# Transposes in place of products for row factors, a token-wise end, and an instruction order from another timing model, in a two-layer hybrid trunk

## The chip, the cores and the metric

The kernel runs on one core of a Trainium2 chip. The metric is the device time of one execution in microseconds, the median of three runs. TensorE is called PE, VectorE DVE, ScalarE ACT, GpSimd POOL, and SyncE, which issues most transfers, SP.

## What is computed

256 tokens of width 1024 pass two layers. Each layer adds half a SwiGLU step, a token mixer of four head groups (forgetting attention, retention, an SSD, HGRN2), another half SwiGLU step, and a gated embedding. The trunk ends with one norm. All of it is float32.

```
h = x
for i in range(DEPTH):
    h = h + 0.5 * swiglu(rmsnorm(h, ffn1_norm[i]), ffn1_w_up[i], ffn1_w_down[i])
    h = h + token_mixer(rmsnorm(h, mix_norm[i]), ...)
    h = h + 0.5 * swiglu(rmsnorm(h, ffn2_norm[i]), ffn2_w_up[i], ffn2_w_down[i])
    gate = sigmoid(rmsnorm(h, ple_norm[i]) @ ple_w_gate[i])
    h = h + gate * (p[i] @ ple_w_proj[i])
return rmsnorm(h, final_norm)
```

## The kernel before

The state `H` stays on the chip with the 1024 channels on the partitions (eight blocks of 128) and the 256 tokens along the free axis. A product in the accuracy that is wanted is made of three: weights and activations are each split into a high part (`wh`, `yh`, a cast on ACT, L160 and L190) and a low part (`wl`, `yl`, a subtraction on DVE, L161 and L191), and PE adds wh·yh, wh·yl and wl·yh into one bank (`prod`, L255; `token_tiles`, L287 to L289, where the tokens are on the partitions of the result).

Weights stream through: SP brings a tile of 128x1024 (`raw`, four buffers), ACT makes `wh` and DVE `wl` (eight buffers each), two tiles ahead of the use (`weight`, `AHEAD`). The banks of PSUM are `bank_p` (two), `bank_m` (two) and `bank_a` (four).

A norm (`Norm`) multiplies `H` by the norm's weights before the split, and takes the factor of each token afterwards: squares on ACT (L204), sums over the channel blocks on POOL (L206, L209), sums over the partitions on PE (L104), nine small steps on DVE for the root (L241 to L250), and then `spread` (L228), two products of the factor's column against the identity matrix, which lay the 256 factors along the free axis of all partitions. Such products in full precision, against the identity or another constant, stand in four more places: L370 (head norms), L731 and L787 (SSD), L812 (forgetting attention). L760, L857, L858 and L863 are real transposes.

In the mixer one projection makes all groups' inputs. `hf` and `hq` of HGRN come first (banks 2336 and 2337 in layer 0, 8815 and 8816 in layer 1), with the statistics of the norm among them, then `hv` and a few columns for gates (banks 2508 and 2509; 8999 and 9000), whose chain of small steps on DVE is `small` (L667 to L687, tiles `sm`), then `fv` (banks 2674 and 2675; 9165 and 9166), then the rest. The parts of the mixer are generators that a planner takes turns with; the order on each engine is then fixed by the tile context's scheduler, which weighs instructions by a timing model of its own. HGRN begins on DVE when the spread factor is there: `hf` and `hq` are scaled (L383), logarithms taken on ACT, a scan (L546), `h` for the carry `dc` (L548, L564), a diagonal product on POOL (L566), and then for each of eight levels exponents (L585 to L596 on DVE, L599 and L600 on ACT), `qt` (L613, DVE) and a product (L621 for the first two, L626 for the others), and masked copies (L637). L653 to L657 make the values. In layer 1 lower bounds add steps (L533, L534, L538, L553).

At the end of layer 1 the gate of the embedding is computed channel block by channel block (`gate`, `gated`, L977 to L980), and the final norm takes squares, statistics, the root, the spread (L228) and one product of `scaled` with the spread factor for each block (L986, L990), and SP writes the result (L991), which the host transposes.

```
    class Norm:
        def spread(self, keep=True):
            for t in range(2):
                mm(self.b[:, 256 + t * P:256 + (t + 1) * P],
                   self.col[:, t:t + 1].broadcast_to([P, P]), ident,
                   start=True, stop=True, skip_group_check=True)
```

Of the kernel before, what the change touches and what calls it, by code (L numbers as in the profile page):

```python
# [47 lines left out]
for _name, _w in (("ffn1", 8), ("mix", 8), ("ffn2", 8), ("ple", 8), ("fin", 8), ("ret", 2),  # L48
                  ("hgrn", 2), ("ssd", 2), ("cw", 16), ("cb", 4), ("lb0", 2), ("lb1", 2),
                  ("sd", 2), ("bias", 8), ("alog", 4)):  # L50
    PAR[_name] = (_n, _w)
    _n += _w
# [4 lines left out]
for _name, _w in (("ident", 128), ("cum", 256), ("cum64", 128), ("m0", 128), ("m1", 128),  # L57
                  ("m2", 128), ("tot", 128), ("cos", 256), ("sin", 256),
                  ("dec", 1024), ("lvl", 6 * 64), ("reset", 512), ("hsel", 2), ("neg", 128)):
    CON[_name] = (_n, _w)  # L60
    _n += _w
# [3 lines left out]
def trunk(ctx, tc, x, pt, par_d, con_d, w_d, ws_d, out):  # L65
# [31 lines left out]
    def flat(t):  # L97
        return t.rearrange("p a b -> p (a b)")

# [79 lines left out]
    class Norm:  # L179
        def __init__(self, split=True):  # L180
            self.split = split
            self.h, self.l, self.sq = [], [], []

        def part(self, c, l, name, first=False):
            if self.split:
                xh, xl = v2(tw("yh", F32R)), v2(tw("yl", F32R))
                for i in range(2):
                    d = 2 * c + i
                    w = prm(l, name, d)
                    A.mul(xh[:, i], H[:, d], w)  # L190
                    V.scalar_tensor_tensor(xl[:, i], H[:, d], w, xh[:, i].bitcast(F32),  # L191
                                           ALU.mult, ALU.subtract)
                    self.h.append(xh[:, i])
                    self.l.append(xl[:, i])
            if not first:
                self.square(c)

        def square(self, c):
            sq = tw("m2")
            if c == 3 and not self.split:  # L200
                for d in range(2):
                    self.last = A.activation(v2(sq)[:, d], H[:, 2 * c + d], AF.Square).ins
            else:
                A.activation(sq, flat(H[:, 2 * c:2 * c + 2]), AF.Square)  # L204
# [15 lines left out]
        def scale(self, keep=True):  # L220
            self.stats()
            self.col = rsqrt(self.b[:, 0:2], 2, 1.0 / D)
            if not keep:
                self.spread(False)

        def spread(self, keep=True):
            for t in range(2):
                mm(self.b[:, 256 + t * P:256 + (t + 1) * P],  # L228
                   self.col[:, t:t + 1].broadcast_to([P, P]), ident,
                   start=True, stop=True, skip_group_check=True)  # L230
            rb = self.b[:, 256:512]
            if keep:
                rb = cp.tile([P, S], F32, name=f"rb{cnt[0]}", tag="rb")
                A.copy(rb, self.b[:, 256:512])
            self.rb = rb.unsqueeze(1).broadcast_to([P, 2, S])
# [112 lines left out]
    def head_norm(o, gate, wname, l, kind, which):  # L348
# [351 lines left out]
    def ssd(l, got, need):  # L700
# [25 lines left out]
        for hp in range(2):  # L726
            br = bank("m")
            for hh in range(2):
                h = 2 * hp + hh
                for t in range(2):  # L730
                    mm(br[:, hh * S + t * P:hh * S + (t + 1) * P],  # L731
                       g[:, t, h:h + 1].broadcast_to([P, P]), K("cum64"), start=True, stop=True,
                       skip_group_check=True)
            br4 = br.rearrange("p (h c e) -> p h c e", h=2, c=4)
            hs = slice(2 * hp, 2 * hp + 2)
            V.tensor_tensor(a0.rearrange("p (h c e) -> p h c e", h=4, c=4)[:, hs], br4,
                            bias[:, hs, 0:4].unsqueeze(3).broadcast_to([P, 2, 4, 64]), ALU.add)
            V.tensor_tensor(a1.rearrange("p (h c e) -> p h c e", h=4, c=2)[:, hs],
                            br4[:, :, 2:4],
                            bias[:, hs, 4:6].unsqueeze(3).broadcast_to([P, 2, 2, 64]), ALU.add)  # L740
# [54 lines left out]
    def fox(l, got, need):  # L795
# [114 lines left out]
    def advance(update, l, name, split=True, first=False):  # L910
        xn = Norm(split)
# [5 lines left out]
    def hpair(c):  # L917
        return flat(H[:, 2 * c:2 * c + 2])

# [18 lines left out]
    for l in range(DEPTH):  # L938
# [8 lines left out]
        ph, pl = split(p_sb)  # L947
        wp = by_row()
# [12 lines left out]
        def gate(c):  # L961
            w = by_column()
            z = v2(tw("m2"))
            if l == DEPTH - 1 and c == 3:
                for m in range(2):
                    b = v2(bank("a"))
                    wh, wl = w[m]
                    for k in range(KD):
                        prod(b[:, 0], wh[:, k], wl[:, k], xn.h[k], xn.l[k], k == 0, k == KD - 1)
                    gated(c, z[:, m:m + 1], b[:, 0:1], m, m + 1)  # L970
            else:
                b = bank("a")
                col_tiles(((b, w),), xn, k_outer=(c == 0))
                gated(c, z, v2(b), 0, 2)

        def gated(c, z, b, m, e):
            V.tensor_mul(z, b, xn.rb[:, m:e])  # L977
            A.activation(z, z, AF.Sigmoid)
            V.tensor_mul(z, z, v2(bp[c])[:, m:e])
            V.tensor_add(H[:, 2 * c + m:2 * c + e], H[:, 2 * c + m:2 * c + e], z)  # L980

        xn = advance(gate, 1, "ffn1", split=(l == 0))
    scaled = [v2(tw("m2")) for _ in range(4)]
    with tc.issue_after(xn.last):
        for d in range(KD):
            A.mul(scaled[d // 2][:, d % 2], H[:, d], prm(1, "fin", d))  # L986
    xn.scale(keep=False)
    for c, o in enumerate(scaled):
        for m, e in ((0, 1), (1, 2)) if c == 0 else ((0, 2),):
            V.tensor_mul(o[:, m:e], o[:, m:e], xn.rb[:, m:e])  # L990
            nc.sync.dma_start(out[:, 2 * c + m:2 * c + e], o[:, m:e])  # L991


def _constants():
# [5 lines left out]
    f["cum64"] = (s <= t) & (s // 64 == t // 64)  # L1000
# [107 lines left out]
```

## Time and profile before

| | |
|---|---|
| median of three runs | 1133.43 us (1131.43 to 1135.0) |
| the profiled execution, its own time | 1132.47 us |
| its span | 1130.7 us |
| granted clock of PE, mean | 0.997 |
| PE busy | 1102.3 us, 97%, 9468 instructions |
| DVE busy | 750.5 us, 66% |
| ACT busy | 568.7 us, 50% |
| POOL busy | 42.1 us, 4% |
| transfers | 193.77 MB, 171 GB/s on average |

A page of the profile gives, engine by engine, the busy share, and in 40 slices the clock that PE was granted. The timeline has one instruction, or several of one kind, to a row: start and duration in us, engine, line, operation, output and inputs, shapes. PE's instructions overlap, so their price is the distance between starts and not the duration. In brackets stands how long the engine was idle before, and what ended that.

### The profile page before, as it was taken

The numbers are of one execution on the slowest core, as the hardware profiler recorded it, in microseconds if no ns is written. First come the engines' busy times: TensorE is split into PE (matmuls) and PEld (weight loads), VectorE is DVE, ScalarE is ACT, GpSimd is POOL, SyncE is SP. The second block draws the span as 40 slices with busy tenths as digits, with TensorE's granted clock in tenths as the row PEclk, the third lists the DMA queues.
The fourth block names the chain that finished last, engine by engine and source line by source line (L and its number), as shares of the span: only waits on it lengthen the run. The fifth ranks groups of instructions, "written<-read, shape, count | busy, mean of one in ns | idle before, by whom it ended". The sixth has DMA issues, their size and how long they took to land.

```text
span 1130.7 us, 22461 instructions
## 1 busy us (share of the span) xinstructions
PE 1102.3 (97%) x9468; PEld 1079.2 (95%) x9468; DVE 750.5 (66%) x1077; ACT 568.7 (50%) x762; POOL 42.1 (4%) x39
## 2 busy tenths in 40 slices
PE   7999999999999999999999999998999999999996
PEld 7999999879899999999999999997899999999996
DVE  6755556798769555556975555577997775555584
ACT  6544444645477444444665444446446854444453
POOL 2000000200001000000100000010000100000011
PEclk9999999999999999999999999999999999999998
DMA  8865566136246665665655566642444576665631
GB/s 265 286 220 182 183 185 185 57 117 196 87 162 221 206 182 186 183 183 156 205 175 184 185 186 186 185 151 61 148 129 150 168 242 184 184 183 183 185 100 38
DMA packets 55302, 193.77 MB, mean 171 GB/s; under 512 B 6560, under 2 KB 7072, under 8 KB 55200
## 3 DMA queue, kind: packets, MB, share of 16 engines
q1 hardware_dynamic: 54480, 191.65, 54.2%
q8 instruction: 74, 1.21, 0.4%
q10 hardware_dynamic: 720, 0.68, 0.2%
q14 instruction: 28, 0.23, 0.1%
HBM read 190.21 MB, written 1.05 MB: 169 GB/s over the span
## 4 chain that ended last, share of the span: by engine, by line
PE 80%; DVE 12%; DMA 3%; ACT 3%; issue 2%; DVEq 0%; SPq 0%; ACTq 0%
PE bank_p L255 27%; PE bank_a L255 26%; PE bank_m L255 21%; DVE wl L161 3%; DMA raw<-w 2%; DVE yl L191 2%; ACT wh L160 1%; DVE H L346 1%; DVE m L344 1%; DVE qt L613 1%; DVE wl L637 1%; ACT yh L190 1%; PE bank_a L104 1%; PE bank_m L695 1%; DMA H<-x 1%
## 5 line engine op out<-in xcount | busy, mean ns | idle before, releaser
L161 DVE TENSOR_TENSOR wl<-raw,wh 128x1024 fp32r<-128x1024 f32 (+2 forms) x360 | 434.2, 1214 | 256.2 <-ACT wh L160 255.5
L160 ACT CAST wh<-raw 128x1024 fp32r<-128x1024 f32 (+2 forms) x360 | 370.9, 1038 | 418.0 <-PE bank_p L255 139.1
L255 PE MATMUL bank_p<-yh,wh 128*128 128x256 f32 x1072 | 306.3, 286 | 6.3 <-ACT wh L160 6.3
L255 PE MATMUL bank_p<-yl,wh 128*128 128x256 f32 x1072 | 304.3, 284 | 0.8 <-DVE yl L191 0.7
L255 PE MATMUL bank_p<-yh,wl 128*128 128x256 f32 x1072 | 303.3, 283 | 0.6 <-DVE wl L161 0.6
L255 PE MATMUL bank_a<-yl,wh 128*128 128x256 f32 x960 | 271.1, 283 | 0.5 <-DVE yl L191 0.5
L255 PE MATMUL bank_a<-yh,wl 128*128 128x256 f32 x960 | 270.8, 282 | 0.0
L255 PE MATMUL bank_a<-yh,wh 128*128 128x256 f32 x960 | 270.6, 283 | 0.0
L255 PEld LDWEIGHTS bank_p<-yh,wh 128*128 128x128 f32 x1072 | 203.6, 190 | 7.4 <-ACT wh L160 6.3
L255 PEld LDWEIGHTS bank_p<-yl,wh 128*128 128x128 f32 x1072 | 203.5, 190 | 2.9 <-DVE yl L191 1.6
L255 PEld LDWEIGHTS bank_p<-yh,wl 128*128 128x128 f32 x1072 | 202.7, 189 | 1.7 <-DVE wl L161 0.8
L255 PE MATMUL bank_m<-yh,wh 128*128 128x256 f32 x720 | 203.3, 282 | 0.0
L255 PE MATMUL bank_m<-yl,wh 128*128 128x256 f32 x720 | 203.0, 282 | 0.0
L255 PE MATMUL bank_m<-yh,wl 128*128 128x256 f32 x720 | 202.3, 282 | 0.0
L255 PEld LDWEIGHTS bank_a<-yl,wh 128*128 128x128 f32 x960 | 181.6, 189 | 1.3 <-DVE yl L191 0.9
L255 PEld LDWEIGHTS bank_a<-yh,wh 128*128 128x128 f32 x960 | 181.3, 189 | 0.8 <-issue 0.8
L255 PEld LDWEIGHTS bank_a<-yh,wl 128*128 128x128 f32 x960 | 181.7, 189 | 0.0
L255 PEld LDWEIGHTS bank_m<-yh,wh 128*128 128x128 f32 x720 | 136.8, 190 | 0.0
L255 PEld LDWEIGHTS bank_m<-yl,wh 128*128 128x128 f32 x720 | 136.6, 190 | 0.0
L255 PEld LDWEIGHTS bank_m<-yh,wl 128*128 128x128 f32 x720 | 136.2, 190 | 0.0
L206 POOL TENSOR_TENSOR m<-m,m 128x512 f32<-128x512 f32 x18 | 27.7, 1539 | 1040.6 <-ACT m L204 902.3
L191 DVE SCALAR_TENSOR_TENSOR yl<-H,par,yh 128x256 fp32r<-128x256 f32 x64 | 45.6, 745 | 12.2 <-ACT yh L190 12.0
(263 smaller groups left out, 803.7 us busy)
## 6 DMA issues: line engine op xcount, KB each, us to landing
raw<-w SPq DMA_DIRECT2D x348, 512.0 KB, 4.2
raw<-ws SPq DMA_DIRECT2D x4, 528.0 KB, 4.3
raw<-w SPq DMA_DIRECT2D x8, 256.0 KB, 5.1
con<-con SPq DMA_DIRECT2D x3, 512.0 KB, 6.7
H<-x SPq DMA_DIRECT2D x4, 256.0 KB, 5.3
out<-m SPq DMA_DIRECT2D x3, 256.0 KB, 2.8
m<-rk SPq DMA_DIRECT2D x8, 64.0 KB, 4.2
m<-rq SPq DMA_DIRECT2D x8, 64.0 KB, 2.5
```

Source lines behind the costliest of these rows:

```text
L104: mm(o[r], lhsT[:, r], rhs, start=start, stop=stop, skip_group_check=True)
L160: A.copy(h[:, cs], r[:, cs])
L161: last_dve[0] = V.tensor_sub(lo[:, cs], r[:, cs], h[:, cs].bitcast(F32)).ins
L190: A.mul(xh[:, i], H[:, d], w)
L191: V.scalar_tensor_tensor(xl[:, i], H[:, d], w, xh[:, i].bitcast(F32), ALU.mult, ALU.subtract)
L206: G.tensor_add(sq, sq, self.sq.pop())
L255: mm(o, wl if n == 2 else wh, xl if n == 1 else xh, start=first and n == 0, stop=last and n == 2, skip_group_check=True)
L344: V.tensor_mul(v2(t), v2(acc[c]), rb)
L346: V.scalar_tensor_tensor(hp, t, 0.5, hp, ALU.mult, ALU.add)
L613: V.tensor_mul(o, q0, e0)
L637: V.copy_predicated(pf[r].rearrange("p (h c n two e) -> p c h n two e", h=8, c=2, two=2, e=L)[:, u, :, :, 1], K("lvl", m, m + 32)[r].rearr ...
L695: mm(b[r, i * S:(i + 1) * S], v[:, 0, cs], pt0(h), start=True, stop=False, skip_group_check=True)
```

## The change

Four things change.

1. A helper `rows` lays a column along the free axis by a transpose of the broadcast column, and takes the place of the product with the identity in `spread` and in the forgetting attention. The head norms transpose too. In the SSD the product with the constant `cum64` goes: the sums that DVE has copied into `bias` are transposed, and the sign of two subtractions on DVE turns.
2. Layer 1 ends in a new function `ending`. Embedding and gate have the tokens on the partitions, with up to 512 columns to a product; `H` is transposed into PSUM (16 transposes); the norm's factor enters as the scale of the sigmoid; ACT sums the squares of a token while it squares; and the output is written by rows. Tokens 0 to 127 come first, then 128 to 255 in pieces of 512, 256 and 256 columns. The weights of the gate come by rows instead of columns, and the eight tiles are all held.
3. The norm's weights for the end come as a tensor of their own (`fin_d`, read on ACT's queue), and `Norm` loses its options.
4. The tile context is made with another timing model for its scheduler, by an option.

```
+    def rows(o, col):
+
+        nc.tensor.transpose(o, col.broadcast_to([P, P]), ident)
...
-        def spread(self, keep=True):
+        def spread(self):
             for t in range(2):
-                mm(self.b[:, 256 + t * P:256 + (t + 1) * P],
-                   self.col[:, t:t + 1].broadcast_to([P, P]), ident,
-                   start=True, stop=True, skip_group_check=True)
...
+                rows(self.b[:, 256 + t * P:256 + (t + 1) * P], self.col[:, t:t + 1])
...
-                mm(b2[:, i * S + t * P:i * S + (t + 1) * P],
-                   re[:, t * 256 + i * P:t * 256 + (i + 1) * P], ident,
-                   start=True, stop=True, skip_group_check=True)
+                nc.tensor.transpose(b2[:, i * S + t * P:i * S + (t + 1) * P],
+                                    re[:, t * 256 + i * P:t * 256 + (i + 1) * P], ident)
...
-                    mm(br[:, hh * S + t * P:hh * S + (t + 1) * P],
-                       g[:, t, h:h + 1].broadcast_to([P, P]), K("cum64"), start=True, stop=True,
-                       skip_group_check=True)
+                    rows(br[:, hh * S + t * P:hh * S + (t + 1) * P], bias[:, h, 4 * t:4 * t + 1])
...
-            mm(bn[:, 256 + t * P:256 + (t + 1) * P], r[:, t:t + 1].broadcast_to([P, P]), ident,
-               start=True, stop=True, skip_group_check=True)
+            rows(bn[:, 256 + t * P:256 + (t + 1) * P], r[:, t:t + 1])
...
-                    mm(b[:, hh * S + t * P:hh * S + (t + 1) * P],
-                       cc[:, 4 * t + h:4 * t + h + 1].broadcast_to([P, P]), ident, start=True,
-                       stop=True, skip_group_check=True)
+                    rows(b[:, hh * S + t * P:hh * S + (t + 1) * P], cc[:, 4 * t + h:4 * t + h + 1])
...
+    def ending(acc, xn, l, ph, pl):
...
+        xg = advance(lambda c: ffn_finish(acc, xn.rb, c), l, "ple")
+        w = by_row(8)
+        pieces = (((0, 512), (512, 1024)), ((0, 512), (512, 768), (768, 1024)))
...
+        def turned(t):
+
+            o = [bank("pm"[u]) for u in range(2)]
+            for d in range(KD):
+                nc.tensor.transpose(o[d // 4][:, (d % 4) * P:(d % 4 + 1) * P],
+                                    H[:, d, t * P:(t + 1) * P], ident)
+            return o
...
+                A.activation(z, bs[n][:, 0:width], AF.Sigmoid, scale=xg.col[:, t:t + 1])
+                V.tensor_mul(z, z, emb[t][u][:, lo:lo + width])
+                V.tensor_add(yy, z, ht[u][:, lo:lo + width])
+                A.activation(z, yy, AF.Square, accum_out=ss[:, n:n + 1])
+                if n < last:
+                    G.tensor_mul(yy, yy, gain[:, cs[0]:cs[1]])
+                if n:
+                    V.tensor_add(ss[:, 0:1], ss[:, 0:1], ss[:, n:n + 1])
+            r = rsqrt(ss[:, 0:1], 1, 1.0 / D)
...
-    with tile.TileContext(nc) as tc, ExitStack() as ctx:
+    with tile.TileContext(nc, schedule_with_timeline_sim=True) as tc, ExitStack() as ctx:
```

The lines shift: L255 becomes L247, L287 to L289 become L279 to L281, L161 L165, L104 L108, L228 L102, L613 L604, L621 L612, L626 L617.

The order moves at three places of interest here. The first is PE around the spread of the mixer's norm in layer 0. `bank_p_2337` is `hq`, `bank_m_2509` one half of `hv`. Before, the spread follows the last products of `hq`, and `hv` comes behind it:

```order
L255 MATMUL bank_p_2337<-yl_2329,wh_2345 128x256
L255 MATMUL bank_p_2337<-yh_2328,wl_2346 128x256
L228 MATMUL bank_a_2434<-con,ry_323_2448 128x128 [waits DVE_49]
L287 MATMUL bank_m_2509<-wh_2351,yh_2292 128x264
L288 MATMUL bank_m_2509<-wl_2352,yh_2292 128x264
```

Now:

```order
L279 MATMUL bank_m_2509<-wh_2357,yh_2328 128x264
L280 MATMUL bank_m_2509<-wl_2358,yh_2328 128x264
L281 MATMUL bank_m_2509<-wh_2357,yl_2329 128x264
L102 MATMUL bank_a_2434<-con,ry_323_2448 128x128 [waits DVE_49]
L279 MATMUL bank_p_2508<-wh_2351,yh_2292 128x264 [waits DVE_49,PE_49]
```

The 24 products of `bank_m_2509` stood behind the spread and stand ahead of it, in part among those of `hf` and `hq` and in part right before the spread; layer 1 has the same.

The second is DVE in layer 0 ahead of `wl_2678`, the low half of the third `fv` tile. `h_356`, `h_375` and `h_377` are the exponents of three HGRN levels, `sm` the small steps for the gates. Before:

```order
L671 TENSOR_SCALAR sm_348_2617<-sm_347_2616 128x16
L594 TENSOR_TENSOR h_356_2648<-lk_2494,hb_2502 128x256
L672 RECIPROCAL sm_348_2617<-sm_348_2617 128x16 [waits DVE_49]
L596 TENSOR_TENSOR h_356_2648<-hb_2502 128x256
L673 TENSOR_TENSOR sm_348_2617<-sm_348_2617,sm_347_2616 128x16 [waits DVE_49]
L161 TENSOR_TENSOR wl_2678<-raw_2676,wh_2677 128x1024 [waits DMAHW1_49]
```

Now:

```order
L585 TENSOR_TENSOR h_356_2648<-lk_2494,hb_2502 128x256 [waits Activation_49]
L587 TENSOR_TENSOR h_356_2648<-hb_2502 128x256
L665 TENSOR_TENSOR sm_349_2618<-sm_348_2617 128x16 [waits DVE_49]
L585 TENSOR_TENSOR h_375_2712<-lk_2494,hb_2502 128x256 [waits Activation_49]
L587 TENSOR_TENSOR h_375_2712<-hb_2502 128x256
L666 TENSOR_SCALAR sm_350_2619<-sm_349_2618 128x16 [waits DVE_49]
L555 COPY dc_2555<-bank_a_2546 128x8 [waits PE_49]
L585 TENSOR_TENSOR h_377_2742<-lk_2494,hb_2502 128x256
L587 TENSOR_TENSOR h_377_2742<-hb_2502 128x256
L668 SCALAR_TENSOR_TENSOR sm_350_2619<-sm_350_2619,sm_349_2618 128x16 [waits DVE_49]
L165 TENSOR_TENSOR wl_2678<-raw_2676,wh_2677 128x1024 [waits DMAHW1_49]
```

Two more levels' exponents and the copy of `dc`, which POOL's product waits for, stand ahead of the low half; three more low halves follow it in a row.

The third is DVE in layer 1 ahead of `wl_9169`, the same tile's low half there. `h_1224` becomes the logarithm with the lower bound, `hb` its scan, `lk` the other side's exponent. Before:

```order
L564 COPY dc_9046<-bank_a_9037 128x8 [waits PE_49]
L161 TENSOR_TENSOR wl_9169<-raw_9167,wh_9168 128x1024 [waits DMAHW4_49]
L538 TENSOR_TENSOR h_1224_8980<-h_1224_8980,h_1223_8971 128x512 [waits Activation_49]
L671 TENSOR_SCALAR sm_1245_9108<-sm_1244_9107 128x16
L161 TENSOR_TENSOR wl_9175<-raw_9173,wh_9174 128x1024 [waits DMAHW5_49]
L546 SCALAR_TENSOR_TENSOR hb_8992<-con,h_1224_8980 128x512 [waits DVE_49]
```

Now:

```order
L537 SCALAR_TENSOR_TENSOR hb_8992<-con,h_1224_8980 128x512 [waits DVE_49]
L668 SCALAR_TENSOR_TENSOR sm_1247_9110<-sm_1247_9110,sm_1246_9109 128x16 [waits DVE_49]
L555 COPY dc_9046<-bank_a_9037 128x8 [waits PE_49]
L544 SCALAR_TENSOR_TENSOR lk_8973<-lk_8973,lb_1007_7296,hb_8992 128x256 [waits DVE_49]
L544 SCALAR_TENSOR_TENSOR lk_8973<-lk_8973,lb_1007_7296,hb_8992 128x256
L576 COPY h_1238_9051<-hb_8992 128x2x64
L577 TENSOR_TENSOR h_1238_9051<-hb_8992 128x2x64
L669 SCALAR_TENSOR_TENSOR sm_1247_9110<-sm_1247_9110,sm_1245_9108 128x16 [waits DVE_49]
L165 TENSOR_TENSOR wl_9169<-raw_9167,wh_9168 128x1024 [waits DMAHW4_49]
L165 TENSOR_TENSOR wl_9175<-raw_9173,wh_9174 128x1024 [waits DMAHW5_49]
```

The logarithm's last step (L538, now L529, two rows further up), the scan, the two steps on `lk` and most of the `small` chain stand ahead of the low half, which was the first thing after `dc`.

## Rows read from the trace of the kernel before

**Rows 1.** The page: busy time by engine; granted clock in 40 slices, in tenths.

```profile
PE 1102.3 (97%) x9468; PEld 1079.2 (95%) x9468; DVE 750.5 (66%) x1077; ACT 568.7 (50%) x762; POOL 42.1 (4%) x39
...
PEclk9999999999999999999999999999999999999998
```

**Rows 2.** What PE waited for: us in total, times, longest.

```profile
PE bank_a L104 <- ACT m L204: 2.2, 4, 0.8
PE bank_a L228 <- DVE ry L250: 2.2, 3, 1.8
PE bank_a L621 <- ACT wh L160: 2.2, 1, 2.2
PE bank_a L626 <- DVE qt L613: 2.0, 3, 0.9
...
PE bank_a L653 <- DVE wl L637: 0.7, 2, 0.4
```

**Rows 3.** Timeline of PE: full-precision groups and the product behind each.

```profile
213.66 0.61 PE L228 MATMUL bank_a<-con,ry 128*128 128x128 f32 x4
214.03 0.37 PE L287 MATMUL bank_m<-wh,yh 128*128 128x264 f32 x1
...
279.74 0.60 PE L760 MATMUL bank_m<-con,wl 128*128 128x128 f32 x4
280.10 0.36 PE L255 MATMUL bank_p<-yh,wh 128*128 128x256 f32 x1
...
295.03 1.05 PE L812 MATMUL bank_m<-con,cc 128*128 128x128 f32 x8
296.01 0.66 PE L695 MATMUL bank_m<-wh,wl 128*64 128x256 f32 x4
```

**Rows 4.** Timeline of PE: the pace of 512 and of 256 columns.

```profile
223.45 0.39 PE L287 MATMUL bank_p<-wh,yh 128*128 128x512 f32 x1
...
225.52 0.40 PE L287 MATMUL bank_p<-wh,yh 128*128 128x512 f32 x1
...
1092.78 0.28 PE L255 MATMUL bank_m<-yh,wl 128*128 128x256 f32 x1
```

**Rows 5.** Timeline of PE and DVE from the last FFN product to the end.

```profile
1087.08 0.28 PE L255 MATMUL bank_a<-yh,wl 128*128 128x256 f32 x1
...
1118.37 0.28 PE L255 MATMUL bank_a<-yh,wl 128*128 128x256 f32 x1
...
1119.59 0.42 DVE L979 TENSOR_TENSOR m<-m,bank_m 128x256 f32<-128x256 f32 x1 [0.48 <-ACT m L978]
...
1121.42 0.16 DVE L241 TENSOR_SCALAR rv<-bank_a 128x2 f32<-128x2 f32 x1 [0.95 <-PE bank_a L104]
...
1122.99 0.16 DVE L250 SCALAR_TENSOR_TENSOR ry<-rt,ry 128x2 f32<-128x2 f32 x1
...
1124.03 2.54 DVE L990 TENSOR_TENSOR m<-m,bank_a 128x256 f32<-128x256 f32 x5 [0.87 <-PE bank_a L228]
```

**Rows 6.** Timeline of PE and DVE in layer 0: L621, then `wl_2678` and its first use.

```profile
227.28 2.15 PE L621 MATMUL bank_a<-qt,kt 128*128 128x128 f32 x16 [1.36 <-DVE qt L613]
...
228.99 1.22 DVE L161 TENSOR_TENSOR wl<-raw,wh 128x1024 fp32r<-128x1024 f32 x1
...
230.85 0.40 PE L288 MATMUL bank_p<-wl,yh 128*128 128x512 f32 x1
```

**Rows 7.** Timeline of DVE and PE in layer 1: `wl_9169`, L538, the scan, the first use, L621.

```profile
777.78 1.22 DVE L161 TENSOR_TENSOR wl<-raw,wh 128x1024 fp32r<-128x1024 f32 x1
778.91 2.38 DVE L538 TENSOR_TENSOR h<-h,h 128x512 f32<-128x512 f32 x1
...
781.17 0.39 PE L288 MATMUL bank_p<-wl,yh 128*128 128x512 f32 x1
782.43 1.21 DVE L546 TENSOR_TENSOR_SCAN hb<-con,h 128x512 f32<-128x512 f32 x1
...
787.62 0.57 PE L621 MATMUL bank_a<-qt,kt 128*128 128x128 f32 x3 [2.16 <-ACT wh L160]
```

More of the change, by code (lines that the diff above doesn't have):

```diff
@@ L47 @@
 _n = 0
-for _name, _w in (("ffn1", 8), ("mix", 8), ("ffn2", 8), ("ple", 8), ("fin", 8), ("ret", 2),
+for _name, _w in (("ffn1", 8), ("mix", 8), ("ffn2", 8), ("ple", 8), ("ret", 2),
                   ("hgrn", 2), ("ssd", 2), ("cw", 16), ("cb", 4), ("lb0", 2), ("lb1", 2),
@@ L56 @@
 _n = 0
-for _name, _w in (("ident", 128), ("cum", 256), ("cum64", 128), ("m0", 128), ("m1", 128),
+for _name, _w in (("ident", 128), ("cum", 256), ("m0", 128), ("m1", 128),
                   ("m2", 128), ("tot", 128), ("cos", 256), ("sin", 256),
@@ L62, with trunk @@
 NCON = _n
-def trunk(ctx, tc, x, pt, par_d, con_d, w_d, ws_d, out):
+def trunk(ctx, tc, x, pt, par_d, con_d, w_d, ws_d, fin_d, out):
     nc = tc.nc
@@ L179, in trunk, with __init__ @@
     class Norm:
-        def __init__(self, split=True):
-            self.split = split
+        def __init__(self):
             self.h, self.l, self.sq = [], [], []
         def part(self, c, l, name, first=False):
[L185 to L194, printed above, removed]
+            xh, xl = v2(tw("yh", F32R)), v2(tw("yl", F32R))
+            for i in range(2):
+                d = 2 * c + i
+                w = prm(l, name, d)
+                A.mul(xh[:, i], H[:, d], w)
+                V.scalar_tensor_tensor(xl[:, i], H[:, d], w, xh[:, i].bitcast(F32),
+                                       ALU.mult, ALU.subtract)
+                self.h.append(xh[:, i])
+                self.l.append(xl[:, i])
             if not first:
@@ L199, in square @@
             sq = tw("m2")
[L200 to L204, printed above, removed]
+            A.activation(sq, flat(H[:, 2 * c:2 * c + 2]), AF.Square)
             if self.sq and c < 3:
@@ L218, in stats, with scale @@
                             c == 0 and d == 0 and t == 0, c == n - 1 and d == 1)
[L220 removed]
+        def scale(self):
             self.stats()
             self.col = rsqrt(self.b[:, 0:2], 2, 1.0 / D)
[L223 to L226 removed]
+        def spread(self):
             for t in range(2):
[L228 to L234 removed]
+                rows(self.b[:, 256 + t * P:256 + (t + 1) * P], self.col[:, t:t + 1])
+            rb = cp.tile([P, S], F32, name=f"rb{cnt[0]}", tag="rb")
+            A.copy(rb, self.b[:, 256:512])
             self.rb = rb.unsqueeze(1).broadcast_to([P, 2, S])
@@ L908, in retention, with advance @@
         return (yield from head_norm(o, got["rg"], "ret", l, "m2", "m"))
-    def advance(update, l, name, split=True, first=False):
-        xn = Norm(split)
+    def advance(update, l, name, first=False):
+        xn = Norm()
         for c in range(4):
@@ L947, in trunk @@
         ph, pl = split(p_sb)
+        if l == DEPTH - 1:
+            ending(acc, xn, l, ph, pl)
+            continue
         wp = by_row()
@@ L962, in gate @@
             w = by_column()
[L963 to L977, printed above, removed]
-            A.activation(z, z, AF.Sigmoid)
[L979 to L991, printed above, removed]
+            z = tw("m2")
+            b = bank("a")
+            col_tiles(((b, w),), xn, k_outer=(c == 0))
+            V.tensor_mul(v2(z), v2(b), xn.rb)
+            A.activation(z, z, AF.Sigmoid)
+            V.tensor_mul(z, z, bp[c])
+            V.tensor_add(hpair(c), hpair(c), z)
+        xn = advance(gate, 1, "ffn1")
 def _constants():
@@ L1069 @@
         tiles.extend(_by_row(a["ple_w_proj"][l]))
-        for c in range(4):
-            tiles.extend(_by_column(a["ple_w_gate"][l][:, c * 256:(c + 1) * 256]))
+        gate = a["ple_w_gate"][l]
+        tiles.extend(_by_row(gate) if l == DEPTH - 1 else _by_column(gate))
         def rep(v):
@@ L1105 @@
     r = bass_utils.run_bass_kernel_spmd(nc, [arrays], core_ids=[0])
-    o = np.asarray(r.results[0]["out"])
-    return np.ascontiguousarray(o.transpose(1, 0, 2).reshape(D, S).T)[None]
+    return np.asarray(r.results[0]["out"])[None]
```

72 lines of the change are left out of this document (65 added, 7 removed).

## The prediction

> **What bounds the kernel now.** The first view is the page: PE is busy 97% of the span, DVE 66% [rows 1]. So time taken off PE is time off the kernel wherever the things that PE needs are ready. The second view, what PE waits for, tells where they are not [rows 2]: apart from the start, the statistics of a norm wait for a square (2.2 us in four waits), the spread of the norm factor for its root (2.2, mostly the last norm), and products in the HGRN mixer for their operands (L621 2.2, L626 2.0, L653 0.7). About 9 us of these lie inside norms and mixers, and can move when instructions are put in another order. The third view is PE's timeline, where the distance of two starts is the price of an instruction. A 128x512 product costs (225.52 - 223.45) / 9 = 0.23 us [rows 4]; 48 products of 128x256 cost 1092.78 - 1087.08 = 5.70, 0.119 each [rows 4, 5]. In full precision a product against a constant takes two passes, a transpose one: L760's four transposes are four instructions and the next product starts 0.36 later, 0.09 a pass; L228's two spreads are four passes in 0.37; L812's four are eight in 0.98, 0.12 a pass [rows 3].
>
> I sum against the profiled execution, 1132.47 us, which is 0.96 below the median of the three runs.
>
> **Transposes for products: -7.0 us.** Outside the ending, L228 loses 14 passes (seven norms, two each), L370 16, L731 16, L787 4 and L812 16: 66 passes. At 0.09 to 0.12 each [rows 3] that is 5.9 to 8.1; I take 0.107, since L731 and L370 stand in groups of eight as L812 does, the others in groups of four. In the mixers they stand between projections, so the time comes off PE's own row. L731 now also waits for DVE's copies into `bias`; in the new order 21 other products (2.5 us) stand between, so I cost that at nothing; without them it would be one wait for a small DVE step, under 0.5 a layer.
>
> **The ending on PE: -1.0.** Now 31.3 us lie between the last FFN product at 1087.08 and the last gate product at 1118.37 [rows 5]. The new one has 24 products of 512 columns for the embedding (5.5), 48 for the gate of tokens 0 to 127 (11.1), the statistics (0.6), 16 transposes of H (16 x 0.11 = 1.8), then 24 of 512 and 48 of 256 columns (5.5 + 5.7): 30.2. Its cover: after the FFN, DVE has five low halves at 1.14 from start to start (5.7), three steps of H (1.8), five splits (2.0) and some 2 in which a POOL step holds it, 11 to 12 in all, and PE asks for the last split 14 us in. Were this gone, the gate would wait some 3 us.
>
> **The tail: -3.1.** Today 8.2 us pass from that last product to the end of the last computation (1124.03 + 2.54 = 1126.57 [rows 5]): three elementwise steps and a square, 0.42 to 0.46 each, statistics, a root of nine small steps (1121.42 to 1123.15), a spread and 2.54 of products. The new tail has 0.3 to the sigmoid, four steps of 0.46, a small add of 0.2, the root 1.76 and 0.85 of products: 5.0. Statistics, spread and most products drop out, as the square now sums per token. I allow 2 to 3.5. The output transfers follow as before.
>
> **The order from the other timing model: +7.7, the term that decides.** In the FFN's steady part nothing moves. In each mixer two things do.
>
> First, 24 products of `hv` (24 x 0.119 = 2.9) now stand before the spread of the norm factor, not behind it. The statistics lose their wait of 0.8 [rows 2], so the spread, and all of the HGRN chain on DVE that begins with it, comes 2.9 - 0.8 = 2.1 later.
>
> Second, DVE does more of that chain before it makes the low half of the next weights. In layer 0 wl_2678 ends at 228.99 + 1.22 = 230.21 and PE takes it at 230.85, with 0.64 to spare [rows 6]. Now two more pairs of L585/L587 (0.34 from start to start) and small steps, 1.7 us, stand before it: 230.21 + 2.1 + 1.7 = 234.0. PE has as much work before that point as ever, so its waits up to there grow by 3.2. Later waits of this mixer (L626, L653; half of their 2.7 [rows 2]) should go, as those products stand further back: +1.8.
>
> In layer 1 wl_9169 was made ahead of L538, from 777.78 to 779.00, and taken at 781.17 [rows 7]. Now L538 (0.6), the scan (1.14), the two steps after it (0.8), two small ones (0.35), twelve of the `small` chain (1.6) and POOL's hold come first; the hold shows as 2.38 in L538 where such a step takes 0.68, so 1.7. Together 6.2: 779.00 + 2.1 + 6.2 = 787.3, and PE stands 6.1 longer. L621's wait of 2.2 [rows 7] goes, because more products lie before it; in its place come about 0.7 for the `small` columns and 1.9 for wl_9315, which stands behind four low halves and a level's rows. Later waits of 1.2 go: 6.1 - 2.2 + 2.6 - 1.2 = +5.3.
>
> At the two FFN starts behind the mixers a low half is taken earlier than it is ready, about 0.8 each, and the start and the norms give back about 1.0: +0.6. Sum 7.7. Bounds: -1 where every new wait is covered and an old one goes, 15 where nothing is given back and the boundaries cost their double.
>
> Sum: 1132.47 - 7.0 - 1.0 - 3.1 + 7.7 = 1129.1, so **1129**, 0.4% under the median.
>
> **A rule against the transposes.** The granted clock is at nine tenths or more in every slice but the last [rows 1], those with L760's transposes among them, which is the level of 2.4 GHz. The Trainium skill, "TensorE: Matmul & The Clock Gate", Part 4, says that transposes on PE don't count as PE-busy in the same way and that the full clock doesn't engage for them. Eight transposes at a time, as the kernel has them now, do not bear it out; sixteen in a row, just ahead of the last gate products, no run here shows, so it is a rival below.
>
> **Rivals.**
> *The order is free or better.* DVE is a third idle over the span [rows 1], and 9 us of PE's waits are there to be won; against it stand the two low halves, with 0.64 and 2.2 in hand. Order -1 to +4: 1120 to 1125, likeliest 1122.
> *The order eats the gain,* when the old waits stay beside the new. Order 11 to 15: 1132 to 1136, no change that can be told.
> *Slower: the HGRN levels queue behind low halves.* In the new order most of the six levels' `qt` steps have one or two low halves (1.2 each) ahead of them on DVE. If PE comes to L617 before they are done, each of six levels in two layers costs about 0.85 more: 7.7 + 10 gives 1139. It decides from 15.5 of order cost in all, and needs PE to have less than 3 us of products between two levels. For it speaks that four low halves stand in a row in both layers; against it, that the levels' products stand further back and DVE catches up.
> *Slower: the clock falls to 1.2 GHz behind the transposes of H.* Then 11.2 us of gate products double: 1140. Against it stands [rows 1].
> *The transposes do not take one pass.* Then 7.0 come back and H's cost 1.8 more: 1138. L760 speaks against it [rows 3].
>
> **How the numbers follow.** A change of 0.3% (3.4 us) is about what a measurement can tell, so faster is under 1130.0 and slower over 1136.8. My forecast (order 4 to 11, 1125 to 1132) has 0.56, of which 0.36 lies under 1130.0; the free order 0.24; the eaten gain 0.14; the levels 0.04; clock and passes 0.02. Faster 0.36 + 0.24 = 0.60; same 0.20 + 0.14 = 0.34; slower 0.06. The range 1120 to 1135.5 takes in the first three but for their far ends.
>
> **What would show it.** Half the instructions in the lines that follow L228, L370, L731, L787 and L812, at 0.09 to 0.12 each; no spread at the end, and about 5 us from the last product to the last step; among PE's waits, L280 for a low half, 3 to 4 in layer 0 and 7 in layer 1, and none for the statistics of the mixer's norm. If PE's waits in the mixers come to no more than now, the order term is wrong and the time is near 1122; if those of L617 exceed those of L280, the first slower rival is right; if gate products start 0.46 apart after the transposes, the second.

## The result and the profile after

The changed kernel takes 1143.15 us (median of 4 runs, 1142.85 to 1148.12); the kernel before takes 1132.64 beside it. The ratio is 1.0094, with a 95% interval of 1.0071 to 1.0117: **slower by 0.9%**, where 1129 had been forecast. The profiled execution took 1142.99 us with a span of 1141.2, 10.5 more than before in both.

The page of the changed kernel (busy time by engine, then the granted clock in 40 slices):

```profile
PE 1101.7 (97%) x9290; PEld 1072.8 (94%) x9290; DVE 748.1 (66%) x1082; ACT 569.3 (50%) x765; POOL 46.1 (4%) x39
...
PEclk9999999999999999999999999998999999999998
```

PE has 178 instructions fewer than in [rows 1] and is busy for the same time, which cannot be if each costs what it did. One slice besides the last now shows an eight in the clock. What PE waits for, in the changed kernel (us in total, times, longest):

```profile
PE bank_p L280 <- DVE wl L165: 6.9, 2, 4.4
PE bank_p L247 <- ACT wh L164: 6.5, 2, 6.2
PE bank_a L247 <- ACT yh L292: 5.9, 5, 1.8
PE bank_p L279 <- DVE h L374: 4.2, 2, 2.1
PE bank_p L247 <- DVE yl L193: 3.1, 4, 1.0
```

The 6.2 is the first weight at the start, as before. All waits of [rows 2] are gone: no statistics, no spread, no HGRN level (L612 and L617 now, L621 and L626 before). In their place stand four larger ones: the products with the third tile of `fv` for its low half (L280, once in each layer), the out-projection for the rounded values of a head (L247 <- yh; 5.4 of the 5.9 in four waits, the rest is one in the first FFN), the products of `hv` for a PSUM bank that DVE still has to empty (L279 <- h), and the first products of a norm for a split (yl). Three smaller ones come to 3.4.

These waits don't all cost their own length alone. Timeline of PE in the changed kernel around the spread of layer 0 (start, duration, instruction, idle time before it):

```profile
218.72 0.38 PE L102 MATMUL bank_a<-con,ry 128*128 128x128 f32 x2
221.20 0.36 PE L279 MATMUL bank_p<-wh,yh 128*128 128x264 f32 x1 [2.09 <-DVE h L374]
221.39 0.28 PE L280 MATMUL bank_p<-wl,yh 128*128 128x264 f32 x1
...
222.78 0.42 PE L279 MATMUL bank_p<-wh,yh 128*128 128x264 f32 x1
223.00 0.42 PE L280 MATMUL bank_p<-wl,yh 128*128 128x264 f32 x1
223.22 0.42 PE L281 MATMUL bank_p<-wh,yl 128*128 128x264 f32 x1
```

Products of 264 columns that started 0.12 apart start 0.22 apart from 222.78 on. Stretches of both kernels (length, busy time and instructions of PE, PEld, DVE, ACT and POOL, then the granted clock, the share of the DMA engines, GB/s); first the changed one:

```profile
220.00:226.00 6.00, 4.80 (x26) 4.74 (x27) 3.13 (x6) 3.84 (x7) 0.00 (x0) 0.72 0.01 3
326.00:334.00 8.00, 6.88 (x44) 6.73 (x45) 3.60 (x15) 5.32 (x16) 0.00 (x0) 0.79 0.01 3
792.00:800.00 8.00, 5.54 (x14) 4.38 (x15) 7.97 (x15) 1.46 (x2) 0.57 (x1) 0.57 0.53 167
```

and the kernel before:

```profile
220.00:226.00 6.00, 5.43 (x37) 3.92 (x36) 5.83 (x13) 2.25 (x7) 2.01 (x1) 1.00 0.00 0
...
792.00:800.00 8.00, 8.00 (x92) 7.31 (x90) 7.42 (x27) 4.38 (x9) 0.00 (x0) 1.00 0.30 90
```

The clock is at 2.4 GHz or at 1.2, so a mean of 0.72 over 6 us is 1.7 us lost, and 0.79 over 8 us is 1.7. In the third stretch 0.57 over 8 us would be 3.4, but there PE still stands in the wait of 4.38 until 794.46, where a slow clock costs nothing. The same stretch by 2 us (length, busy time of PE, clock, DMA):

```profile
792.00:794.00 2.00, 0.00 (x0) 0.66 0.00 0
794.00:796.00 2.00, 1.54 (x4) 0.50 0.32 41
796.00:798.00 2.00, 2.00 (x6) 0.50 0.81 293
798.00:800.00 2.00, 2.00 (x7) 0.63 0.98 336
```

That is 0.77 + 1.0 + 0.74 = 2.5 us lost while PE works. Together **5.9 us** are lost to the clock in the mixers, at three waits; in the kernel before it is 0. PE counts as busy while it works at half speed, so this is 5.9 of the 7.4 us by which the fall of its busy time (0.6) is short of the 8.0 that the forecast took off PE.

### The profile page after: what moved, and what is told of

Same layout as the page of the kernel before. It is cut to its first block, busy times and chain, and to the rows that moved or that the text cites. A ratio compares the mean times of both kernels' runs of the same rounds, so it can differ in the third digit from the quotient of the medians.

```text
span 1141.2 us, 22094 instructions
## 1 busy us (share of the span) xinstructions
PE 1101.7 (97%) x9290; PEld 1072.8 (94%) x9290; DVE 748.1 (66%) x1082; ACT 569.3 (50%) x765; POOL 46.1 (4%) x39
## 4 chain that ended last, share of the span: by engine, by line
PE 86%; DVE 6%; ACT 3%; DMA 3%; issue 1%; SPq 0%; ACTq 0%; DVEq 0%
PE bank_p L247 32%; PE bank_a L247 27%; PE bank_m L247 21%; DVE wl L165 2%; DMA raw<-w 2%; ACT wh L164 1%; PE bank_a L108 1%; PE bank_a L617 1%; PE bank_m L813 1%; DMA H<-x 1%; PE bank_m L686 1%; DMA par<-par 0%; PE bank_m L102 0%; DVE m L971 0%; ACT m L973 0%
## 5 line engine op out<-in xcount | busy, mean ns | idle before, releaser
L165 DVE TENSOR_TENSOR wl<-raw,wh 128x1024 fp32r<-128x1024 f32 (+2 forms) x360 | 442.3, 1239 | 254.6 <-ACT wh L164 253.9
L247 PE MATMUL bank_p<-yh,wh 128*128 128x256 f32 x1064 | 303.2, 286 | 7.8 <-ACT wh L164 6.5
L247 PE MATMUL bank_p<-yl,wh 128*128 128x256 f32 x1064 | 301.1, 284 | 3.1 <-DVE yl L193 3.1
L247 PE MATMUL bank_p<-yh,wl 128*128 128x256 f32 x1064 | 300.8, 284 | 1.0 <-DVE wl L165 0.8
L247 PE MATMUL bank_a<-yh,wh 128*128 128x256 f32 x896 | 247.3, 283 | 5.9 <-ACT yh L292 5.9
L247 PE MATMUL bank_a<-yl,wh 128*128 128x256 f32 x896 | 252.3, 284 | 0.0
L247 PE MATMUL bank_a<-yh,wl 128*128 128x256 f32 x896 | 251.5, 283 | 0.0
L247 PEld LDWEIGHTS bank_p<-yh,wh 128*128 128x128 f32 x1064 | 201.8, 190 | 9.2 <-ACT wh L164 6.7
L247 PEld LDWEIGHTS bank_p<-yl,wh 128*128 128x128 f32 x1064 | 201.6, 190 | 4.6 <-DVE yl L193 3.9
L247 PEld LDWEIGHTS bank_p<-yh,wl 128*128 128x128 f32 x1064 | 201.0, 189 | 2.9 <-DVE wl L165 1.6
L247 PE MATMUL bank_m<-yh,wh 128*128 128x256 f32 x712 | 200.6, 282 | 0.0
L247 PE MATMUL bank_m<-yl,wh 128*128 128x256 f32 x712 | 200.2, 282 | 0.0
L247 PE MATMUL bank_m<-yh,wl 128*128 128x256 f32 x712 | 200.0, 282 | 0.0
L247 PEld LDWEIGHTS bank_a<-yh,wh 128*128 128x128 f32 x896 | 167.7, 190 | 6.7 <-ACT yh L292 6.7
L247 PEld LDWEIGHTS bank_a<-yl,wh 128*128 128x128 f32 x896 | 170.3, 190 | 0.9 <-issue 0.3
L247 PEld LDWEIGHTS bank_a<-yh,wl 128*128 128x128 f32 x896 | 170.1, 190 | 0.0
L247 PEld LDWEIGHTS bank_m<-yh,wh 128*128 128x128 f32 x712 | 135.1, 190 | 0.0
L247 PEld LDWEIGHTS bank_m<-yl,wh 128*128 128x128 f32 x712 | 135.0, 190 | 0.0
L247 PEld LDWEIGHTS bank_m<-yh,wl 128*128 128x128 f32 x712 | 134.6, 190 | 0.0
L192 ACT ACTIVATE yh<-H,par 128x256 fp32r<-128x256 f32 x64 | 29.0, 501 | 34.0 <-DVE H L338 24.7
```

The source lines that it names most:

```text
L165: last_dve[0] = V.tensor_sub(lo[:, cs], r[:, cs], h[:, cs].bitcast(F32)).ins
L247: mm(o, wl if n == 2 else wh, xl if n == 1 else xh, start=first and n == 0, stop=last and n == 2, skip_group_check=True)
```

## The experiments

Ratios are to runs of the kernel before beside them on the same chip. In kernels with added lines the line numbers run some lines ahead; the tiles in the rows tell which is meant.

**The option, and everything but the option.** The first two kernels split the change at its last line:

```
-    with tile.TileContext(nc) as tc, ExitStack() as ctx:
+    with tile.TileContext(nc, schedule_with_timeline_sim=True) as tc, ExitStack() as ctx:
```

alone on the kernel before, and left out of the changed one; the third and fourth take the two other parts alone, as they stand in the diff.

> The kernel before with the option alone. Theory A (the order costs, the rest pays as it was summed): the order costs about 10.5 + 11 = 21 us, so 1150 to 1154. Theory B (the order costs no more than the 7.7 that was forecast, and the transposes or the ending do not pay): 1136 to 1141.

> The changed kernel without the option. Theory A: the transposes save 7, the ending 4, nothing is given back: 1121 to 1123. Theory B: 1133 to 1137, the new end or the transposes give nothing.

> The kernel before with the transposes alone, old order model, old end. Theory A: 66 passes and those of the last spreads, 7 us off: 1125 to 1127. Theory B, the transposes keep two passes or are hidden: 1131 to 1133.

> The kernel before with the new ending alone, products in place of the transposes except those of H, old order model. Theory A: 1.0 on PE and 3.1 in the tail: 1128 to 1130. Theory B, the ending gives nothing: 1132 to 1135.

| kernel | median us | ratio, 95% interval | difference at 1133 us |
|---|---|---|---|
| option alone | 1152.49 | 1.0162, 1.0147 to 1.0177 | +18.4 |
| all but the option | 1128.56 | 0.9953, 0.9936 to 0.9969 | -5.3 |
| transposes alone | 1130.35 | 0.9973, 0.9956 to 0.9989 | -3.1 |
| ending alone | 1128.65 | 0.9956, 0.9939 to 0.9973 | -5.0 |

The forecasts for the option and for the ending held; all but the option and the transposes alone came out between their two theories. The option is what makes the change slower: +18.4 on the old code and, from 0.9953 to 1.0094, +16.0 on the new (spans 1125.0 and 1141.2). To see where, the product with the same count can be looked up in both traces, all but the option against all of it (counted are products of 256 columns and more on all 128 rows, before the one named; times of their starts, us):

| product | what lies before it | without option | with | step |
|---|---|---|---|---|
| 400th | start, first products of FFN1 | 58.90 | 60.90 | +2.0 |
| 1660th | FFN1 of layer 0 | 211.13 | 212.73 | -0.4 |
| 2520th | mixer of layer 0, start of FFN2 | 354.29 | 363.80 | +7.9 |
| 5830th | FFN2, gate, FFN1 of layer 1 | 751.73 | 760.59 | -0.7 |
| 6800th | mixer of layer 1, start of FFN2 | 911.78 | 927.55 | +6.9 |
| last | FFN2, ending | 1115.59 | 1131.67 | +0.3 |

So 14.8 of the 16 us lie in the mixers and the starts of the second FFNs behind them, and the rest of the FFNs doesn't move, as forecast. The 16 are a net sum. Without the option PE has two waits of its own at the starts of the second FFNs, 2.40 at 343.59 and 2.31 in layer 1 (L247 <- wl, 4.7), and a stretch at 1.2 GHz behind the first (0.72 over 343 to 349), which the option's order does not have. Against a kernel without the option in which these starts are covered (1122.05 us, below), the option costs 21 us.

The transposes alone brought less than half of their 7.0. Their waits of PE have an entry that neither [rows 2] nor the forecast has:

```profile
PE bank_m L257 <- DVE wl L165: 4.9, 2, 2.5
```

and their DVE around the start of the second FFN in layer 0 shows it:

```profile
339.25 2.51 DVE L195 SCALAR_TENSOR_TENSOR yl<-H,par,yh 128x256 fp32r<-128x256 f32 x2
341.68 1.75 DVE L165 TENSOR_TENSOR wl<-raw,wh 128x1024 fp32r<-128x1024 f32 x1
343.35 0.87 DVE L195 SCALAR_TENSOR_TENSOR yl<-H,par,yh 128x256 fp32r<-128x256 f32 x2
```

With the transposes even the old timing model chose another order: the low half that the first products need now stands behind six splits, two of which took 2.51 instead of the 0.87 to 0.89 of the others. (Whether the shorter instructions or the new dependency of L731 on `bias` moved it, no run separates.) Two waits of 2.3 and 2.5 us, and a stretch at 1.2 GHz in layer 1's mixer, are what the transposes gave back.

**Undoing two places of the option's order at the head of the mixer.** The first kernel holds the products of `hv` behind the spread, as in the old order (`turn` is the spread's last transpose):

```
-                token_tiles([b[:, 0:HIW] for b in bh], w, xn, 4 * n, (n == 0, n == 0), n == 1)
+                with tc.issue_after(xn.turn):
+                    token_tiles([b[:, 0:HIW] for b in bh], w, xn, 4 * n, (n == 0, n == 0), n == 1)
```

the second fetches `fv`'s weights before the HGRN gates are written out, so that their low halves come ahead of the gates on DVE; the third has both:

```
             got["hq"] = scaled(bb, o=keep("hq"))
+            while len(queue) < 6 and wi[0] < len(units):
+                fetch()
```

> The changed kernel, with the 48 products of hv (L279 to L281) held behind the spread's two transposes on TensorE in both mixers; the option stays. Theory A (the head of the mixer is late, and what waits behind it is tied to the spread through VectorE): the spread moves ahead of 24 products (24 x .12 = 2.9 us), less the wait for the statistics that these products had filled (about 1 us), the two waits for the drain of the p banks (2.34 us each) go because 24 products now lie behind the spread, but the waits for the low halves (2.60 and 4.45 us) end only as much sooner as the spread does. Gain 1 to 2.9 us a layer, and 1.7 us where a stretch at 1.2 GHz goes: 1136 to 1140 us. Rival B (the products only change places: what TensorE does not wait in the drain it waits at the low halves): 1142 to 1144 us. Rival C (the drain waits are lost time by themselves, all of it comes back, with the clock): 1135 us or less.

> The changed kernel, with the weights of fv fetched ahead of the mixer's first scaled product, so that their low halves stand ahead of the HGRN gates on VectorE; the option stays, the spread stays behind the products of hv. Theory A (the low halves, held behind the HGRN and SSD values, cost what the two waits show, and the stretch at 1.2 GHz behind the second of them): the waits of 2.60 and 4.45 us go and with the second 3.4 us of clock, some 10 us, and 2 to 4 us come back where the HGRN products (L612, L617) or the out-projection wait next: 1133 to 1138 us, and the drain waits of 2.3 us stay. Rival B (the HGRN values, now behind two low halves of 1.2 us, hold TensorE as long): 1141 to 1144 us.

> The changed kernel with both edits, the spread ahead of hv and fv's low halves ahead of the HGRN gates. Theory A (these two places in each layer are most of the 14.6 us that the option costs; the waits of the out-projection, 1.90, 1.17, 1.88 and 1.07 us, follow from heads that come late): 1129 to 1134 us, and the out-projection's waits shrink. Rival B (the out-projection's waits are the order's own, and stay): 1134 to 1138 us. Rival C (HGRN's chain sets the end of the mixer whatever stands where): 1140 us or more.

Measured: 1146.44 us (1.0123, 1.0102 to 1.0143), 1140.34 (1.0066, 1.0047 to 1.0085) and 1140.81 (1.0069, 1.0051 to 1.0088), against 1.0094 with neither. All three of my theories A were too hopeful. Waits of PE with the spread first:

```profile
PE bank_p L247 <- DVE yl L193: 6.7, 4, 2.6
...
PE bank_p L280 <- DVE wl L165: 4.5, 2, 4.3
```

The wait for the banks (the drain, 4.2) is gone and the low halves cost 2.4 less, but the first products of the mixers' norms now wait 2.63 and 2.60 for splits instead of 0.96 and 0.90: the products of `hv` were what filled that wait too (work that PE can do while an operand is late is called its cover here). HGRN's first level waits 1.5 where it had not. With 9.5 us lost to the clock instead of 5.9, counted in the same way, the kernel is no faster. Rival B had the kind right, though not the place, and its time was too low as well: there is one piece of cover, the products of `hv`, and two waits that need it.

With the low halves first both L280 waits are gone, 6.9 us, and the clock costs 3.4 instead of 5.9. Only 3 us of these 9.4 reach the span (1138.0). New waits took part of the room, among them 1.7 and 0.9 for HGRN levels and 0.9 for the product of the levels with `hv`. The gain is in the direction of theory A, though the interval overlaps that of the changed kernel. With both edits the out-projection's waits stay (6.8 us with the one in the first FFN), as rival B said, and the spread's edit takes away again what it gives. The time falls in rival C's range, but HGRN's chain is not what PE waits for there: its entries come to 1.4 us, those for splits to 5.6.

**The out-projection.** This wait is the largest that the forecast had not seen. Timeline of PE in the changed kernel, layer 0:

```profile
324.35 0.38 PE L102 MATMUL bank_m<-con,ry 128*128 128x128 f32 x2
324.65 0.63 PE L108 MATMUL bank_m<-con,m 128*64 128x2 f32 x16
327.12 0.74 PE L247 MATMUL bank_a<-yh,wh 128*128 128x256 f32 x4 [1.83 <-ACT yh L292]
```

L102 here spreads SSD's norm factor; DVE's step, ACT's rounding and the product at 327.12 follow from it. In the kernel without the option the same two transposes stand 27 products earlier in PE's row, with HGRN's products still to come as cover (at 313.63, behind the 2247th product against the 2274th). The edit holds the later dozens of HGRN's 48 products back (the lines that set `scored` and `turned` are left out):

```
+                    behind = (None, "scored", "scored", "turned")[q] if n == 0 else None
+                    while behind and behind not in got:
+                        yield False
+                    with tc.issue_after(got[behind]) if behind else ExitStack():
+                        accumulate(acc, w, *Y[m], n == 0, n == 3, (2 * q, 2 * q + 1))
```

(`scored` is the softmax head's last score product, `turned` SSD's last spread transpose.)

> The changed kernel, with the option; of HGRN's 48 out-projection products on TensorE (L247, banks a) the second and third dozen are held behind the last score product of the softmax head, the last dozen behind the SSD norm's two transposes (L102). Theory A (under the option these two steps stand behind all of HGRN's products, so that nothing is left to cover the chain from them to the SSD head's rounded values): the waits of 1.90 and 1.88 us for yh go, and the stretch at 1.2 GHz behind the first of them (1.7 us), some 4 to 5.5 us: 1137.5 to 1139.5 us. Rival B (the wait moves on to the retention or softmax head's values, which stay late): 1141 to 1144 us.

> The same out-projection edit on top of fv's low halves ahead of the HGRN gates (that alone: 1140.3 us). Theory A: both places pay, 1134.5 to 1137 us. Rival B (the out-projection's end is set by the heads however its products stand): 1139 to 1142 us.

On the changed kernel alone: 1143.08 us (1.0087, 1.0072 to 1.0101), no gain. With the low halves first: 1136.43 (1.0027, 1.0018 to 1.0036), 4.4 us under the low halves alone by the ratios, the intervals apart. In both, L247's wait for yh is 2.5 in place of 5.9 and 6.3, each with 0.5 to 0.6 in the first FFN. But in the former the scheduler also moved HGRN's first level ahead of `fv`'s products in layer 1:

```profile
796.73 1.65 PE L616 MATMUL bank_a<-qt,kt 128*128 128x128 f32 x6 [6.07 <-ACT kt L595]
```

where the changed kernel had waited 4.38 for the low half, so that run tells nothing of the out-projection's price. The latter does: both places pay, as theory A said. Of the 16 us that the option costs, 7.6 come back (1.0094 to 1.0027). By the table's products this kernel is still 2.5 us late at the 400th, 5.0 more come in layer 0's mixer and 2.7 in layer 1's (its profiled execution is 10.6 us behind that of all but the option). The start and the drains, still 4.2 us among its waits, are in that; I did not try to remove them on this kernel, so their price in it is read from the trace alone.

**The start of the second FFN, without the option.** Two more weight tiles are fetched before the mixer's sum is added to H, on all but the option, and on the transposes alone:

```
+        while len(queue) < 4 and wi[0] < len(units):
+            fetch()
         xn = advance(lambda c: V.tensor_add(hpair(c), hpair(c), acc[c]), l, "ffn2")
```

> All of the change but the option, with two more weight tiles fetched before the mixer's sum is added to H, so that a low half stands between the first two of these additions on VectorE. Theory A (without the option the shorter transposes moved that low half behind six splits, and the start of the second FFN waits for it): the waits of 2.56 and 2.46 us fall to some .8 us each, as in the kernel before, and the stretch at 1.2 GHz behind the first of them goes (1.7 us): 1122 to 1125 us, against 1128.6 us. Rival B (the splits that now stand behind the low half are waited for instead): 1127 to 1129 us.

> The kernel before with the transposes alone, and with the low half put ahead at the start of the second FFN. Theory A (the transposes are worth the 7.0 us of the forecast once the new wait there is gone, less 1.7 us for the stretch at 1.2 GHz behind HGRN's first level in the second layer, if it stays): 1125 to 1127 us. Rival B (the 3.4 us of the transposes alone is all there is): 1128 to 1130 us.

Measured: **1122.05 us** (0.9907, 0.9888 to 0.9927) and 1125.90 (0.9937, 0.9923 to 0.9951). Theory A holds in both. The former beats both kernels, by 10.5 us and by 21. The latter is -7.1 us: with that wait covered, the transposes are worth what was forecast. (The two lines on the kernel before, where that low half already stands ahead of the splits, were not run.)

**The clock.** The fastest kernel still has one stretch at 1.2 GHz, behind a wait for HGRN's first level in layer 1. Its PE there:

```profile
779.08 0.40 PE L279 MATMUL bank_p<-wh,yh 128*128 128x512 f32 x1
781.64 3.05 PE L612 MATMUL bank_a<-qt,kt 128*128 128x128 f32 x16 [2.16 <-ACT wh L164]
784.62 0.80 PE L280 MATMUL bank_p<-wl,yh 128*128 128x512 f32 x1
```

The edit puts work into the wait (a dependency, left out here, keeps it behind the products that come before):

```
+            if L == 128 and l == 1:
+                for _ in range(18):
+                    z = nc.tensor.transpose(bs[:, 0:P], ident, ident).ins
...
```

> The fastest version so far (all of the change but the option, low half ahead in the second FFN; 1122.05 us), with 18 extra transposes of the identity on TensorE in the second layer, in the 2.33 us in which it waits for HGRN's first level (L612); they write a bank that L612 then overwrites. Theory A (a TensorE that stands idle there is what the clock falls behind): the granted clock stays at 2.4 GHz, L612's 16 passes take about 2.1 us, as in the kernel before, not 3.05, and the time falls by up to 1.7 us, to 1120.3 us. Rival B (something else lowers the clock): the stretch stays, 1122 us. Rival C (the extra passes end after HGRN's values are there): 1122.5 to 1124 us.

```profile
779.07 2.13 PE L614 MATMUL bank_a<-con 128*128 128x128 f32 x18
781.40 2.15 PE L622 MATMUL bank_a<-qt,kt 128*128 128x128 f32 x16 [0.21 <-ACT wh L164]
783.48 0.49 PE L285 MATMUL bank_p<-wl,yh 128*128 128x512 f32 x1
785.75 1.11 PE L627 MATMUL bank_a<-qt,kt 128*64 128x64 f32 x16 [1.78 <-DVE qt L610]
786.79 0.80 PE L286 MATMUL bank_p<-wh,yl 128*128 128x512 f32 x1
787.38 0.63 PE L279 MATMUL bank_p<-wh,yh 128*128 128x512 f32 x1
```

The first level's 16 passes now take 2.15 and not 3.05, but the next level, which comes sooner, waits 1.78 for its operand, and the clock falls behind that one (512 columns 0.43 apart from 787.38). Time 1121.76 us (0.9900, 0.9886 to 0.9915): the same. The stretch moved by one wait, and this is no proof that idleness alone makes it: in the transposes with the covered start PE waits 2.17 in the very same place, and the passes there take 2.15 without any filling.

## Why the prediction was wrong

The sum's terms, one by one:

- **Transposes, -7.0.** Right as a price, wrong as a gain. In the kernel with the transposes and the covered start a norm's two spreads are followed by the next product 0.13 later (212.90 to 213.03), where the four passes of L228 took 0.37 [rows 3]: 0.12 for each pass saved. H's sixteen take 1.66 in all (1118.85 to 1120.51), 0.104 each, and with the start of FFN2 covered the kernel gains 7.1. Alone they gained 3.1, since the old scheduler's order changed and two waits of 2.3 and 2.5 came up. The forecast priced the edit and the option as if only the option moved anything.
- **Ending on PE, -1.0, and tail, -3.1.** Right. From the last FFN product to the last gate product it is now 1131.67 - 1101.12 = 30.55 against 31.29 in [rows 5], -0.74. From there to the end of the span it is 1141.2 - 1131.67 = 9.5 against 1130.7 - 1118.37 = 12.3: -2.8. Alone the ending gave -5.0 (3.1 to 6.9), against 4.1 forecast.
- **Order, +7.7: the step that failed.** It is +16 on the new code (21 against the covered kernel) and +18.4 on the old, beyond the bound of 15. By its steps:
  - The low halves: forecast 3.2 in layer 0 and 6.1 in layer 1, measured 2.53 and 4.38 (the 6.9 of the waits). Mechanism and place right, sizes a quarter and two fifths too large. DVE was not earlier than forecast: its four low halves of layer 0 (L165) start at 235.76, so the first ends at about 237.0, where 234.0 was forecast. PE waited less since the drain (2.1), and in layer 0 the slow clock (1.7), had held it before. The 1.9 for wl_9315 and the 0.7 for the `small` columns don't show among the waits.
  - What would be given back: L621's wait in layer 1 is gone, as I said, and so are L626's and L653's, which I had counted with 1.4 and 1.2 of their 2.7. L621's 1.36 in layer 0 went too, which I had not counted.
  - "In each mixer two things do" was the error; there were more. The bank drain behind the spread (4.2 us in two) follows from the first thing I named: I counted what 24 products ahead of the spread delay, not that the first 12 of them (214.03 to 215.59 in the kernel before) had also covered DVE's emptying of the two `p` banks that the next product writes. The out-projection (5.4 in four) I never looked at, since no wait stood there before: the new order had used up its cover, 27 products of HGRN, before SSD's spread. The start adds 2.0.
  - And the clock: 5.9 us. I named a fall of the clock as a rival, but behind the transposes of H, not behind waits. The kernel before has waits of 1.36 and 2.16 with no fall behind them [rows 6, 7], and the sum took every wait at its length alone.
- **What the tests in the forecast said.** "If those of L617 exceed those of L280": L617 does not wait at all, so the slower rival by the levels is not what happened. It was slower by another way, to which I gave nothing: several new waits beside each other, three of them with slow products at them.

**The rule against the transposes.** The Trainium skill, "TensorE: Matmul & The Clock Gate", Part 4, says that the full clock does not engage for transposes. The changed kernel has sixteen in a row, and the products behind them:

```profile
1118.85 0.60 PE L945 MATMUL bank_p<-con,H 128*128 128x128 f32 x4
...
1120.51 0.48 PE L937 MATMUL bank_a<-wh,yh 128*128 128x512 f32 x1
1120.83 0.39 PE L938 MATMUL bank_a<-wl,yh 128*128 128x512 f32 x1
1121.05 0.39 PE L939 MATMUL bank_a<-wh,yl 128*128 128x512 f32 x1
1121.29 0.39 PE L937 MATMUL bank_a<-wh,yh 128*128 128x512 f32 x1
```

The gate products are 0.23 apart as in [rows 4], not 0.46. That rival fell, and here the trace speaks against the rule: sixteen transposes did not bring the clock down, nor did the eighteen in the last experiment (2.13 us). A longer row no run shows. The forecast's "eight transposes at a time" was a misreading: the longest row in the kernel before is four (L760 [rows 3]).

## What to carry to other kernels

A scheduler's option is not an edit with a price: it redistributes cover, and the places to look at are those where nothing waits today. For every wait that a new order removes, ask which independent products filled it, and what these same products had been covering before. A cheaper instruction can be a change of order too, as the transposes were here even under the old timing model, so a small saving should be tried together with a look at what it moves; two lines that put one low half ahead brought 4 to 5 us, more than the transposes had without them.

## What the runs showed of the hardware that was not expected

A wait of PE of about 2 us in the middle of dense work can be followed by a stretch at 1.2 GHz that costs another 1.7 us, nearly doubling its price; in the changed kernel the stretches at three waits (2.09, 1.83, 4.38) cost 1.7, 1.7 and 2.5, and its four runs show mean granted clocks of 0.987 to 0.992, the lowest in the longest run. That these stretches belong to the waits is read from where they stand; no run took the clock's fall away by itself. It is not settled by the length of the wait. The wait for HGRN's first level in layer 1 is 2.16 or 2.17 in six of these kernels; in the kernel before it was not followed by a slow stretch,

```profile
787.62 2.15 PE L621 MATMUL bank_a<-qt,kt 128*128 128x128 f32 x16 [2.16 <-ACT wh L160]
789.70 0.50 PE L288 MATMUL bank_p<-wl,yh 128*128 128x512 f32 x1
```

nor in the ending alone or the transposes with the covered start, while in the transposes alone, in all but the option and in the fastest kernel it was. What decides between them stays open. A wait can even be short: with the low halves first and the out-projection's edit a stretch begins at 298.5 behind one of 0.71, products of 256 columns then 0.21 apart,

```profile
296.29 0.71 PE L890 MATMUL bank_m<-m,m 64*128 64x128 f32 x4 [0.71 <-DVE wh L893]
...
298.74 0.42 PE L247 MATMUL bank_p<-yh,wl 128*128 128x256 f32 x1
298.95 0.41 PE L247 MATMUL bank_p<-yh,wh 128*128 128x256 f32 x1
```

while the changed kernel has the same products behind a wait of 0.72 (L883 at 297.54) and stays 0.12 apart.
